# A two-block fp32 transformer kernel: norm squares behind the splits at the start, operand sums issued amid the last block's first tiles, and a compressed-key tile laid out for unit-step reads

## The chip, the cores and the metric
The kernel runs on one core of one Trainium2 chip. The metric is the device time of one execution in microseconds, the median of three runs.

## The reference
One sequence of 512 tokens with 1024 features, fp32, passes through two blocks.
```
first_block:
x = x + 0.5 * swiglu(rms_norm(x, norm_ffn1), ffn1_w1, ffn1_w3, ffn1_w2)
x = x + hybrid_mixer(rms_norm(x, norm_mix), ...)
x = x + memory_attention(rms_norm(x, norm_mem_q), rms_norm(mem, norm_mem_kv), ...)
x = x + 0.5 * swiglu(rms_norm(x, norm_ffn2), ...)
x = rms_norm(x, norm_out)
...
swiglu(h, w1, w3, w2) = (silu(h @ w1) * (h @ w3)) @ w2
rms_norm(x, g) = x * rsqrt(mean(x * x) + EPS) * g
```
The second block runs sparse attention with 16 heads in 4 groups (over compressed, selected and windowed keys), a matrix-memory LSTM and a cross-attention side by side, merges them through an output projection, and ends with a normed feed-forward network (FFN). The compressed keys come from a small MLP over blocks of 32 successive tokens, one block every 8 tokens, 31 blocks.

## The kernel before
**Products.** Activations lie transposed, features on the 128 partitions and the 512 tokens along the row: x is eight tiles x[d]. An fp32 product with full accuracy is made of three products of split operands (`mm3`): ACT casts the operand to a rounded high part (`copy_hi`, L93, with a gain L94), DVE takes the rest (`lo`, L98, L99), and PE computes high·high, high·low and low·high. `Ctx.split` issues both; with `pin` they keep program order on their engines. The order of all else is set by the tile scheduler, by priorities that follow the order of issue. Tiles come from pools: `q` (split operands, weights), `b` (8 scratch tiles) and eight PSUM banks (`ps`).

**Weights.** `Stream` loads raw weight tiles of 512 KB in the order of their use and splits them ahead. `Stream.start` loads x and the first four weight tiles together, in four pieces of two feature chunks each: per piece x[d], the columns of four raw tiles (L249), x[d + 1]; the first two of the odd ones go through ACT's queue, all else through SP's. It returns one function per piece that splits its columns. `tile_block` calls these, and `next_pair` splits x[d] and x[d + 1] with the norm's gain; the norm's own scale (one over the root of the mean square of a token) is applied behind the products, from the row tile `rb`.

**Norm.** `Norm.add_fast` squares a tile on ACT (L284) and adds it to an accumulator on DVE (L286). `finish` sums over partitions by products with ones, reads the sums into `nv` on DVE (L314), takes the root on POOL (L322) and builds diagonals on DVE (L329); products with ones spread them over the partitions, and ACT copies the result to `rb` (L334).

**FFN up.** `UpPairs` forms pairs of products by Strassen's scheme, with seven products of half size in place of eight; it needs sums and differences of the operands' halves, which `Operands.sums` makes (two scalings on ACT, L374 and L375, three adds on DVE, L377 to L379, then a split, for each of four pairs of tiles). The first tiles need no sums: `UpPairs.first` computes four plain products in the first FFN, chunk by chunk. In the last block it computes six, each in two halves of 256 tokens, since the second half of the residual stream isn't ready when the first is; `run` issues `ops.sums()` behind `first`.

**Ahead of the last FFN.** `product(h, d)` is the output projection of half h, `resid` and `resid2` form the norm and the residual sums and split the operands of the half; `rows(t, j)` transposes x back to token rows on PE (four transposes into a bank, L118), copies the bank on ACT (L2266) and stores it to `xtd`, for the end of the kernel. The object `halves` in `first` walks through these stages; its last call is the transposes of the second half.

**Compression.** `Nsa.take_c` multiplies a projected PSUM tile by the token scale `rb` and writes it into the tile `cz` for k or v (L1550, eight multiplies each); `compress` runs the MLP's first layer, 16 `k.mm` for each of k and v, whose moving operand is every eighth column of `cz` from column c on (4 groups by 31 blocks). These fp32 products are not split, and the trace shows two records for each, 64 in all.

Of the kernel before, what the change touches and what calls it, by code (L numbers as in the profile page):

```python
# [11 lines left out]
AF = mybir.ActivationFunctionType  # L12
# [3 lines left out]
P = 128  # L16
S = 512
NT = S // P
D = 1024
KD = D // P  # L20
# [16 lines left out]
class Ctx:  # L37
# [70 lines left out]
    def mm(self, out, a, b, start, stop, skip=False):  # L108
        return self.nc.tensor.matmul(out, a, b, start=start, stop=stop, skip_group_check=skip)  # L109
# [22 lines left out]
class Stream:  # L132
# [20 lines left out]
    def add(self, key, src, split=True):  # L153
        self.order.append((key, src, split))
# [79 lines left out]
    def start(self, x, xT, gains):  # L234

        k = self.k
        raw, hl = [], []
        m = 4
        for n in range(m):
            raw.append(k.rawp.tile([P, 1024], F32, tag="raw", name=k.nm("raw")))  # L240
            hl.append((k.q([P, 1024], F32R), k.q([P, 1024], F32R)))
            self.hl[n] = hl[n]
        self.nd = self.ns = self.nsum = m
        k.nc.scalar.dma_start(gains, k.a["gains"])
        for d in range(0, KD, 2):
            c = slice(d * P, (d + 2) * P)
            k.nc.sync.dma_start(x[d], xT[d])
            for n in range(m):
                (k.nc.scalar if d == 0 and n % 2 == 0 else k.nc.sync).dma_start(raw[n][:, c], self.order[n][1][:, c])  # L249
                if n == 1:  # L250
                    k.nc.sync.dma_start(x[d + 1], xT[d + 1])
        self._dma()
        return [lambda c=slice(d * P, (d + 2) * P): [k.split(hl[n][0][:, c], hl[n][1][:, c], raw[n][:, c], pin=True) for n in range(m)]
                for d in range(0, KD, 2)]

    SUMS = 2

    def next(self, key):
        self.prefetch(self.AHEAD)
        assert self.order[self.n][0] == key, (key, self.order[self.n][0])  # L260
        r = self.hl.pop(self.n)
        self.n += 1
        return r
# [9 lines left out]
class Norm:  # L273
# [4 lines left out]
        self.acc = k.b([P, cols])  # L278
        self.first = True

    def add_fast(self, x):
        k = self.k
        t = self.acc if self.first else k.b([P, self.cols])
        k.nc.scalar.activation(t, x, AF.Square)  # L284
        if not self.first:
            k.nc.vector.tensor_add(self.acc, self.acc, t)  # L286
        self.first = False
# [59 lines left out]
class Operands:  # L347
# [8 lines left out]
        self.k = k  # L356
        self.b1, self.b2, self.th, self.tl, self.x = [], [], [], [], []

    def add(self, x1, x2, g1, g2, c=slice(0, S), pin=False):

        k = self.k
        if c.start == 0:
            self.b1.append(k.q([P, 2, S], F32R))
            self.b2.append(k.q([P, 2, S], F32R))
            self.x.append((x1, x2, g1, g2))
        j = next(j for j in range(KD // 2) if self.x[j][0] is x1)
        for b, x, g in ((self.b1[j], x1, g1), (self.b2[j], x2, g2)):
            k.split(b[:, 0, c], b[:, 1, c], x[:, c], g, pin)

    def sums(self):  # L370
        k, nc, H = self.k, self.k.nc, self.H
# [45 lines left out]
class UpPairs:  # L417
# [93 lines left out]
    def first(self):  # L511


        k, halves = self.k, self.halves
        ps = []
        if halves is None:
            for n in range(self.side):
                ps.append((k.ps(), self.weights(0, "ab"[n // 2])[n % 2]))
            for kk in range(KD):
                for p, w in ps:  # L520
                    self.plain(p, w, ks=[kk])
            return [p for p, _ in ps]
        for n in range(self.side):
            ps.append((k.ps(), self.weights(n // 4, "ab"[n // 2 % 2])[n % 2]))
            if n in (1, 2):
                halves = halves()
            self.plain(*ps[n], slice(0, 256))
        for n, (p, w) in enumerate(ps):
            self.plain(p, w, slice(256, 512))
            if n == 1:  # L530
                last = self.finish()
            if n == 3:
                self.rb = last()
        halves()
        return [p for p, _ in ps]

    def run(self):
        k = self.k
        steps = up_steps()
        which = {1: "x", 6: "x", 7: "x", 4: "x", 5: "y", 3: "y", 2: "z"}  # L540
        done = {"a": "a", "b": "b", 4: "a22", 3: "s34", 5: "s12", 2: "f1"}
        last = None
        pend = []
        ps0 = self.first()
        self.ops.sums()
        for n, num in steps:
            if ps0:
                ps, ps0 = ps0[:2], ps0[2:]
                pend.append((n, num, ps))
            elif num in ("a", "b"):  # L550
                ps = [k.ps(), k.ps()]
                for m, (p, w) in enumerate(zip(ps, self.weights(n, num))):
                    self.plain(p, w)
                    if m == 0 and last is None and self.rb is None:
                        last = self.finish()
                pend.append((n, num, ps))
            else:
                first = num in (1, 5, 2)
                if first:
                    self.bank[n, which[num]] = k.ps([P, 2, 256])  # L560
                self.product(n, num, self.bank[n, which[num]], first)
                self.take(n, num)
            if self.rb is None and last is not None:
                self.rb = last()
            if self.rb is not None:
                while pend:
                    m, ab, ps = pend.pop(0)
                    self.out_plain(2 * m + (ab == "b"), *ps)
                if (n, 11) in self.c:
                    z = self.c.pop((n, 11))  # L570
                    self.out(2 * n, 0, z, z)
            if n == NF // 2 - 1:
                k.W.AHEAD = 2
                if num == 1:
                    self.ops.b1 = None
                if num == 4:
                    self.ops.th = self.ops.tl = None
            if num in done:
                self.w.pop((n, done[num]), None)
        k.W.AHEAD = Stream.AHEAD  # L580
        self.ops.b2 = None
        return self.g
# [39 lines left out]
    norm.add(x[d])  # L622


def next_pair(x, ops, d, gain, norm, pin=False):
    ops.add(x[d], x[d + 1], gain[:, d : d + 1], gain[:, d + 1 : d + 2], pin=pin)
    if not pin:
        norm.add(x[d])
        norm.add(x[d + 1])

# [875 lines left out]
class Nsa:  # L1506
# [34 lines left out]
    def take_c(self, which, c):  # L1541
        def take(p):
            k, nc = self.k, self.k.nc
            if c == 0:
                self.cz[which] = k.q([P, 4, 256])
            z = self.cz[which]
            for j in range(2):
                r = slice(64 * j, 64 * j + 64)
                for par in range(2):
                    nc.vector.tensor_mul(z[64 * par : 64 * par + 64, 2 * c + j, :], p[r, par::2], self.rb[r, par::2])  # L1550
        return take

    def compress(self):

        k, nc = self.k, self.k.nc
        w1, acc = {}, {}
        for which in "kv":
            w1[which] = [k.q([P, 1024]) for _ in range(2)]
            for hf in range(2):
                nc.sync.dma_start(w1[which][hf], k.a["cmp_w1_" + which][hf])  # L1560
        for which in "kv":
            acc[which] = k.b([P, P])
            self.pe_sum(nc.gpsimd if which == "k" else nc.vector, which, w1[which], acc[which])
        for which in "kv":
            z = self.cz.pop(which)
            w = w1.pop(which)
            p = k.ps([P, 4, 32])
            for c in range(16):
                k.mm(p[:, :, :31], w[c // 8][:, (c % 8) * P : (c % 8 + 1) * P], z[:, :, c : c + 241 : 8], c == 0, c == 15)
                yield 216  # L1570
            pb = k.ps([P, 2])
            k.mm(pb[:, 0:1], acc.pop(which), k.ones[:, 0:1], True, True)
            hid = self.hidden(p, pb)
            yield 3000
            self.second(which, hid)
            yield 1000
# [309 lines left out]
def tile_block(ctx: ExitStack, tc: tile.TileContext, aps, out):  # L1886
    nc = tc.nc
    k = Ctx(ctx, tc, aps)
# [38 lines left out]
    G = {n: gains[:, i, :] for i, n in enumerate(GAINS)}  # L1927
    x = [k.half() for d in range(KD)]
    k.warm(12)
    first = W.start(x, aps["xT"], gains)  # L1930
# [10 lines left out]
    k.rb = k.const([P, S], "rb")  # L1941
    ops, norm = Operands(k), Norm(k)
    for d in range(0, KD, 2):
        first[d // 2]()
        next_pair(x, ops, d, G["norm_ffn1"], norm, True)
    for d in range(KD):
        norm.add_fast(x[d])
    x.clear()

    up = UpPairs(k, ("ffn1_w1", "ffn1_w3"), ops, lambda norm=norm: norm.finish(None, k.rb), 4)  # L1950
# [1 line left out]
    g = up.run()  # L1952
# [3 lines left out]
    xs, norm = [], Norm(k)  # L1956
    for d, p in ffn_down(k, "ffn1_w2", g):
        t = k.b()
# [28 lines left out]
    xs, norm = [], Norm(k)  # L1987
# [35 lines left out]
    ops, norm = Operands(k), Norm(k)  # L2023
# [10 lines left out]
    g = up.run()  # L2034
# [5 lines left out]
    xs, norm, norm5 = [], Norm(k), Norm(k)  # L2040
    for d, p in ffn_down(k, "ffn2_w2", g):
        t = k.b()
# [451 lines left out]
```

## Time and profile before
| | before |
|---|---|
| median of three runs | 2230.64 us (2230.48 to 2231.96) |
| profiled execution | 2232.27 us |
| its span | 2230.5 us |
| mean granted clock of TensorE | 0.995 |
| busy: PE, weight loads, DVE, ACT, POOL | 2192.0, 1911.3, 1515.2, 1021.4, 297.7 us |
| DMA | 235.73 MB, 106 GB/s in mean |

PE is the matrix engine, DVE the vector engine, ACT the scalar engine, POOL the general one, and SP issues most DMAs. A busy time counts records on the engine; PE's is near the span, so time is gained only where PE waits or where its records become shorter. Where records overlap at their ends, a count in a stretch includes those cut by its edges.

### The profile page before, as it was taken

What the parts mean: (1) busy time and instruction counts of PE and PEld (TensorE: products, weight loads), DVE (VectorE), ACT (ScalarE), POOL (GpSimd) and SP (SyncE); (2) the same over time, 40 slices, a digit from 0 to 9 for tenths busy, and PEclk for the clock granted to TensorE, in tenths of its full rate; (3) what the DMA queues carried; (4) which work ended last, traced back from release to release, by engine and by line L of the source; (5) the groups of instructions that cost most, each with busy time, mean ns of one, the idle gap of its engine ahead of it and who ended that gap; (6) DMA issues with size and microseconds to landing.
All of it is one profiled execution on the core that took longest, in us unless ns stands there. A gap on an engine that the chain in (4) does not pass through costs nothing.

```text
span 2230.5 us, 32697 instructions
## 1 busy us (share of the span) xinstructions
PE 2192.0 (98%) x12746; PEld 1911.3 (86%) x12746; DVE 1515.2 (68%) x2601; ACT 1021.4 (46%) x1790; POOL 297.7 (13%) x347
## 2 busy tenths in 40 slices
PE   8999999999999999999999999999999999899998
PEld 6999888878888889999888878887777799899987
DVE  7898644656866667888445945626888747798832
ACT  6455523545344544545224443315666635554620
POOL 0000021301234030000230000213334200000000
PEclk9999999999999999999999999999999999999999
DMA  5233524212333332335133223531111442233431
GB/s 175 95 114 99 180 66 140 74 64 83 124 124 104 114 109 81 104 114 187 54 118 133 67 91 100 180 122 58 58 48 58 142 152 95 76 114 104 160 105 38
DMA packets 79076, 235.73 MB, mean 106 GB/s; under 512 B 9028, under 2 KB 12868, under 8 KB 78920
## 3 DMA queue, kind: packets, MB, share of 16 engines
q1 hardware_dynamic: 74456, 225.99, 30.9%
q10 hardware_dynamic: 4464, 7.65, 0.9%
q8 instruction: 100, 1.64, 0.3%
q14 instruction: 56, 0.46, 0.1%
HBM read 216.30 MB, written 17.30 MB: 105 GB/s over the span
## 4 chain that ended last, share of the span: by engine, by line
PE 88%; DVE 6%; ACT 2%; issue 2%; POOL 1%; DMA 0%; SPq 0%; ACTq 0%; DVEq 0%; POOLq 0%
PE ps L109 86%; PE ps L118 2%; DVE q L98 1%; ACT q L1755 1%; DVE nx L1753 1%; POOL hr L322 1%; DVE q L99 0%; ACT q L93 0%; DMA raw<-in_ffn_w_dram 0%; DVE b L286 0%; DVE q L2245 0%; DVE q L1653 0%; DVE hn L723 0%; DVE nr L1757 0%; POOL q L1760 0%
## 5 line engine op out<-in xcount | busy, mean ns | idle before, releaser
L109 PE MATMUL ps<-q,q 128*128 128x256 f32 (+3 forms) x11736 | 2119.0, 341 | 19.9 <-ACT q L94 8.9
L109 PEld LDWEIGHTS ps<-q,q 128*128 128x128 f32 x11736 | 1803.9, 191 | 254.2 <-ACT q L94 9.1
L98 DVE TENSOR_TENSOR q<-raw,q 128x1024 fp32r<-128x1024 f32 (+2 forms) x385 | 430.3, 1135 | 101.8 <-ACT q L93 54.7
L93 ACT CAST q<-raw 128x1024 fp32r<-128x1024 f32 (+2 forms) x385 | 349.6, 938 | 111.3 <-PE ps L109 88.6
L93 ACT CAST q<-q 128x1024 fp32r<-128x1024 f32 (+1 forms) x188 | 164.8, 892 | 139.2 <-PE ps L109 66.0
L98 DVE TENSOR_TENSOR q<-q,q 128x1024 fp32r<-128x1024 f32 (+1 forms) x188 | 189.5, 1025 | 57.1 <-ACT q L93 49.7
L293 POOL TENSOR_TENSOR b<-q 128x512 f32<-128x512 f32 x32 | 36.9, 1156 | 709.4 <-DVE q L1960 302.5
L468 ACT ACTIVATE b<-b 128x256 f32<-128x256 f32 x108 | 44.9, 417 | 134.5 <-DVE b L467 134.5
L1755 ACT ACTIVATE q<-ps,nx 128x128 f32<-128x128 f32 (+3 forms) x128 | 67.5, 531 | 56.9 <-DVE nx L1753 25.7
L1760 POOL TENSOR_SCALAR q<-q,nr 128x128 f32<-128x128 f32 (+3 forms) x128 | 72.0, 569 | 143.7 <-DVE nr L1758 99.7
L459 ACT COPY b<-ps 128x512 f32<-128x512 f32 x81 | 47.3, 584 | 90.1 <-PE ps L109 90.0
L118 PE MATMUL ps<-ident,q 128*128 128x128 f32 x512 | 81.6, 275 | 6.7 <-POOL q L1760 2.6
L118 PEld LDWEIGHTS ps<-ident,q 128*128 128x128 f32 x512 | 61.9, 141 | 25.0 <-POOL q L1760 8.0
L98 DVE TENSOR_TENSOR q<-ps,q 128x512 fp32r<-128x512 f32 x112 | 74.1, 682 | 11.2 <-ACT q L93 10.8
L94 ACT ACTIVATE q<-q,gains 128x512 fp32r<-128x512 f32 (+1 forms) x48 | 30.4, 648 | 105.2 <-DVE q L1960 34.6
L297 POOL TENSOR_TENSOR b<-b,b 128x512 f32<-128x512 f32 (+1 forms) x49 | 70.6, 1447 | 2.8
L93 ACT CAST q<-ps 128x512 fp32r<-128x512 f32 x112 | 62.7, 593 | 16.8 <-PE ps L109 11.6
L1753 DVE TENSOR_REDUCE nx<-ps 128x1 f32<-128x384 f32 (+3 forms) x96 | 56.0, 583 | 0.0
L99 DVE SCALAR_TENSOR_TENSOR q<-q,gains,q 128x512 fp32r<-128x512 f32 (+1 forms) x48 | 35.5, 753 | 19.2 <-ACT q L94 19.1
L322 POOL TENSOR_TENSOR sr<-ss,mhalf 128x4 f32<-128x4 f32 x8 | 8.1, 1008 | 296.5 <-DVE ss L1387 187.3
L469 DVE TENSOR_TENSOR q<-b,b 128x256 f32<-128x256 f32 x81 | 33.8, 421 | 19.4 <-ACT b L468 19.0
L322 POOL TENSOR_TENSOR or<-ov,mhalf 128x1 f32<-128x1 f32 x4 | 2.2, 548 | 334.4 <-DVE ov L2345 334.4
(264 smaller groups left out, 1417.7 us busy)
## 6 DMA issues: line engine op xcount, KB each, us to landing
raw<-in_ffn_w_dram SPq DMA_DIRECT2D x100, 512.0 KB, 4.3
raw<-in_w_ffn_in_dram SPq DMA_DIRECT2D x44, 512.0 KB, 3.8
raw<-in_w_gm_dram SPq DMA_DIRECT2D x24, 512.0 KB, 3.3
raw<-in_ffn_w2a_dram SPq DMA_DIRECT2D x22, 512.0 KB, 4.4
raw<-in_w_ffn_down_dram SPq DMA_DIRECT2D x22, 512.0 KB, 4.4
raw<-in_w_out_dram SPq DMA_DIRECT2D x16, 512.0 KB, 3.6
raw<-in_w_mk_dram SPq DMA_DIRECT2D x8, 512.0 KB, 3.6
raw<-in_w_mv_dram SPq DMA_DIRECT2D x8, 512.0 KB, 4.0
```

What stands on the lines that cost most here:

```text
L93: return self.nc.scalar.copy(out, in_)
L98: return self.nc.vector.tensor_sub(out, in_, hi.bitcast(F32))
L99: return self.nc.vector.scalar_tensor_tensor(out, in_, gain, hi.bitcast(F32), op0=ALU.mult, op1=ALU.subtract)
L109: return self.nc.tensor.matmul(out, a, b, start=start, stop=stop, skip_group_check=skip)
L118: return self.nc.tensor.transpose(out, in_, self.ident[:n, :n])
L293: k.nc.gpsimd.tensor_tensor(t, x, x, op=ALU.mult)
L297: k.nc.gpsimd.tensor_tensor(self.acc, self.acc, t, op=ALU.add)
L459: self.k.nc.scalar.copy(z, bank)
L468: nc.scalar.activation(t, t, AF.Silu)
L1753: nc.vector.tensor_reduce(mx, s.rearrange("p j b t -> p b j t"), axis=AX.XY, op=ALU.max, negate=True)
L1755: nc.scalar.activation(pr[b][:, :n], s[:, :, c, :], AF.Exp, bias=mx[:, c : c + 1], accum_out=sm[:, c : c + 1])
L1760: nc.gpsimd.tensor_scalar(pr[b][:, :n], pr[b][:, :n], r[:, c : c + 1], 1.0, op0=ALU.mult, op1=ALU.mult)
```

## The change
Four pieces of code change.

- At the start, the first two feature chunks become pieces of their own (cuts 0-1, 1-2, 2-4, 4-6, 6-8); `next_pair` hands a function down through the argument `pin`, so that the second chunk's weight columns are split between the two x tiles. The squares of the first norm are pinned, which puts them in program order, behind all splits.
- `UpPairs.first` of the last block calls the transposes behind the second half of tile 0 and drops its weights tile by tile.
- `ops.sums()` of the last block is issued behind the second half of tile 1.
- `cz` has the layout [4, 8, 32] in place of [4, 256]: token 8n + r lies at row r, place n. The multiplies write with a step of 32 elements, and the first layer reads 31 successive ones.

```diff
@@ Stream.start
-        for d in range(0, KD, 2):
-            c = slice(d * P, (d + 2) * P)
-            k.nc.sync.dma_start(x[d], xT[d])
+        cuts = [(0, 1), (1, 2), (2, 4), (4, 6), (6, 8)]
+        for a, b in cuts:
+            c = slice(a * P, b * P)
+            k.nc.sync.dma_start(x[a], xT[a])
             for n in range(m):
-                (k.nc.scalar if d == 0 and n % 2 == 0 else k.nc.sync).dma_start(raw[n][:, c], self.order[n][1][:, c])
-                if n == 1:
-                    k.nc.sync.dma_start(x[d + 1], xT[d + 1])
+                (k.nc.scalar if a == 0 and n % 2 == 0 else k.nc.sync).dma_start(raw[n][:, c], self.order[n][1][:, c])
+                if n == 1 and b == a + 2:
+                    k.nc.sync.dma_start(x[a + 1], xT[a + 1])
...
@@ Operands.add
-        for b, x, g in ((self.b1[j], x1, g1), (self.b2[j], x2, g2)):
-            k.split(b[:, 0, c], b[:, 1, c], x[:, c], g, pin)
+        k.split(self.b1[j][:, 0, c], self.b1[j][:, 1, c], x1[:, c], g1, pin is not None)
+        if pin is not None:
+            pin()
+        k.split(self.b2[j][:, 0, c], self.b2[j][:, 1, c], x2[:, c], g2, pin is not None)
@@ UpPairs.first
-        for n, (p, w) in enumerate(ps):
+        for n in range(self.side):
+            p, w = ps[n]
             self.plain(p, w, slice(256, 512))
+            ps[n] = p, None
+            if n % 2 == 1:
+                del w, self.w[n // 4, "ab"[n // 2 % 2]]
+            if n == 0:
+                halves()
             if n == 1:
                 last = self.finish()
+                self.ops.sums()
             if n == 3:
                 self.rb = last()
-        halves()
@@ UpPairs.run
-        self.ops.sums()
+        if self.halves is None:
+            self.ops.sums()
@@ Nsa.take_c
-                self.cz[which] = k.q([P, 4, 256])
+                self.cz[which] = k.q([P, 4, 8, 32])
...
-                    nc.vector.tensor_mul(z[64 * par : 64 * par + 64, 2 * c + j, :], p[r, par::2], self.rb[r, par::2])
+                    nc.vector.tensor_mul(z[64 * par : 64 * par + 64, 2 * c + j].rearrange("p r n -> p n r"),
+                                         p[r, par::2].rearrange("p (n r) -> p n r", r=8),
+                                         self.rb[r, par::2].rearrange("p (n r) -> p n r", r=8))
@@ Nsa.compress
-                k.mm(p[:, :, :31], w[c // 8][:, (c % 8) * P : (c % 8 + 1) * P], z[:, :, c : c + 241 : 8], c == 0, c == 15)
+                k.mm(p[:, :, :31], w[c // 8][:, (c % 8) * P : (c % 8 + 1) * P], z[:, :, c % 8, c // 8 : c // 8 + 31], c == 0, c == 15)
@@ tile_block
-        first[d // 2]()
-        next_pair(x, ops, d, G["norm_ffn1"], norm, True)
+        first[d]()
+        next_pair(x, ops, d, G["norm_ffn1"], norm, first.get(d + 1, lambda: None))
     for d in range(KD):
-        norm.add_fast(x[d])
+        norm.add_fast(x[d], True)
```

The scheduler turns this into an order on each engine. ACT at the start of the program, before (raw are weight tiles, q_80 to q_82 tiles of x):
```order
L249 DMA raw_97<-in_ffn_w_dram 128x256
L249 DMA raw_103<-in_ffn_w_dram 128x256
L284 ACT_TABLE_LOAD
L284 ACTIVATE b_141<-q_80 128x512
L284 ACTIVATE b_199<-q_80 128x512
L284 ACTIVATE b_202<-q_81 128x512
L284 ACTIVATE b_205<-q_81 128x512
L284 ACTIVATE b_208<-q_82 128x512
L93 CAST q_98<-raw_97 128x256
L93 CAST q_101<-raw_100 128x256
L284 ACTIVATE b_211<-q_82 128x512
L93 CAST q_104<-raw_103 128x256
```
and now:
```order
L250 DMA raw_97<-in_ffn_w_dram 128x128
L250 DMA raw_103<-in_ffn_w_dram 128x128
L93 ACT_TABLE_LOAD
L93 CAST q_98<-raw_97 128x128
L93 CAST q_101<-raw_100 128x128
L93 CAST q_104<-raw_103 128x128
L93 CAST q_107<-raw_106 128x128
L94 ACTIVATE q_154<-q_80,gains 128x512
L93 CAST q_98<-raw_97 128x128
L93 CAST q_101<-raw_100 128x128
L93 CAST q_104<-raw_103 128x128
L93 CAST q_107<-raw_106 128x128
```
The five squares (L284) ahead of the first cast are gone, the casts are half as wide, and the first scaling of x comes behind the first four.

DVE at the read of the first norm's sum (`nv`; q_384 and q_388 belong to the third of four operand sums, b_473 and b_485 are the diagonals), before:
```order
L378 TENSOR_TENSOR q_384<-b_380,q_384 128x256
L379 TENSOR_TENSOR q_384<-b_381,q_384 128x512
L314 TENSOR_SCALAR nv_445<-ps_440 128x4
L329 TENSOR_SCALAR b_473<-ident,nr_447 128x128 x3
L98 TENSOR_TENSOR q_389<-q_384,q_388 128x1024
```
and now:
```order
L383 TENSOR_TENSOR q_384<-b_380,q_384 128x256
L384 TENSOR_TENSOR q_384<-b_381,q_384 128x512
L317 TENSOR_SCALAR nv_457<-ps_452 128x4
L332 TENSOR_SCALAR b_485<-ident,nr_459 128x128 x4
L98 TENSOR_TENSOR q_389<-q_384,q_388 128x1024
```
The read stands behind the same sum as before, and all four diagonals now come in one piece.

ACT at the last block's operand sums (b_18175 and b_18077 are their first scaled operands, b_18144 and the like the transposed rows, rb the norm's scale), before:
```order
L93 CAST q_17914<-raw_17781 128x1024
L334 COPY rb<-ps_18084 128x256
L334 COPY rb<-ps_18091 128x256
L2266 COPY b_18144<-ps_18143 128x512
L2266 COPY b_18152<-ps_18151 128x512
L2266 COPY b_18160<-ps_18159 128x512
L2266 COPY b_18168<-ps_18167 128x512
L374 ACTIVATE b_18175<-q_16201,gains 128x512
L375 ACTIVATE b_18176<-q_17070,gains 128x512
```
and now:
```order
L2281 COPY b_18022<-ps_18021 128x512
L2281 COPY b_18030<-ps_18029 128x512
L379 ACTIVATE b_18077<-q_16213,gains 128x512
L380 ACTIVATE b_18078<-q_17082,gains 128x512
L379 ACTIVATE b_18089<-q_17082,gains 128x512
L380 ACTIVATE b_18090<-q_17085,gains 128x512
L379 ACTIVATE b_18101<-q_17085,gains 128x512
L380 ACTIVATE b_18102<-q_17088,gains 128x512
L93 CAST q_18085<-q_18081 128x1024
L379 ACTIVATE b_18113<-q_17088,gains 128x512
L380 ACTIVATE b_18114<-q_17091,gains 128x512
L337 COPY rb<-ps_18176 128x256
```
The copies of the norm's scale stood ahead of the row copies and the scalings; now the scalings and the first split of a sum stand ahead of the scale.

## Rows read from the trace of the kernel before
**Rows 1.** The page's busy times by engine, and its chain by engine
```profile
PE 2192.0 (98%) x12746; PEld 1911.3 (86%) x12746; DVE 1515.2 (68%) x2601; ACT 1021.4 (46%) x1790; POOL 297.7 (13%) x347
...
PE 88%; DVE 6%; ACT 2%; issue 2%; POOL 1%; DMA 0%; SPq 0%; ACTq 0%; DVEq 0%; POOLq 0%
```

**Rows 2.** Waits of PE: what released it, total us, times, mean us
```profile
PE ps L109 <- ACT q L94: 8.9, 1, 8.9
PE ps L109 <- DVE q L98: 3.9, 4, 2.5
```

**Rows 3.** Timeline, 0 to 45: start, us, engine, line, operation, out<-in, count [idle before <-releaser]
```profile
11.50 0.69 ACT L93 CAST q<-raw 128x256 fp32r<-128x256 f32 x2
14.48 29.38 PE L109 MATMUL ps<-q,q 128*128 128x512 f32 x120 [8.92 <-ACT q L94]
```

**Rows 4.** Timeline of PE, 1862 to 1935, the last block's start
```profile
1886.35 6.00 PE L109 MATMUL ps<-q,q 128*128 128x256 f32 x48
1901.55 16.93 PE L109 MATMUL ps<-q,q 128*128 128x512 f32 x96 [0.24 <-ACT b L2266]
1921.17 0.74 PE L109 MATMUL ps<-q,q 128*128 128x256 f32 x4 [2.69 <-ACT q L93]
1924.46 10.73 PE L109 MATMUL ps<-q,q 128*128 128x256 f32 x69 [2.54 <-DVE q L98]
```

**Rows 5.** Windows and lines by form of PE, 1432.6 to 1446.9 (compression)
```profile
1432.60:1446.90 14.30, 14.30 (x64) 12.44 (x63) 4.34 (x5) 2.20 (x3) 1.43 (x2) 1.00 0.64 207
L109 PE MATMUL ps<-q,q 128*128 128x124 f32 x32 | 9.0, 398 | 0.0
```

**Rows 6.** Lines by form of PE, 1470 to 1500
```profile
L109 PE MATMUL ps<-q,q 128*128 128x512 f32 x134 | 30.5, 389 | 0.0
```

**Rows 7.** Chain, 0 to 60: start us, us, what
```profile
1.66 5.06 DMA raw<-in_ffn_w_dram
```

**Rows 8.** Lines by form, 0 to 24.5: count | busy us, mean ns | idle before
```profile
L98 DVE TENSOR_TENSOR q<-raw,q 128x256 fp32r<-128x256 f32 x16 | 5.8, 417 | 0.0
L99 DVE SCALAR_TENSOR_TENSOR q<-q,gains,q 128x512 fp32r<-128x512 f32 x8 | 5.6, 745 | 0.0
L94 ACT ACTIVATE q<-q,gains 128x512 fp32r<-128x512 f32 x8 | 5.3, 714 | 0.0
L93 ACT CAST q<-raw 128x256 fp32r<-128x256 f32 x16 | 5.3, 398 | 0.0
```

**Rows 9.** Windows: us, PE, PEld, DVE, ACT, POOL busy (records), PEclk, DMA share, GB/s
```profile
16.00:18.00 2.00, 2.00 (x6) 1.56 (x5) 2.00 (x6) 2.00 (x5) 0.00 (x0) 0.50 0.99 360
1926.00:1930.00 4.00, 4.00 (x23) 4.00 (x23) 3.95 (x5) 0.97 (x2) 0.00 (x0) 0.56 0.37 132
```

**Rows 10.** Timeline, 36 to 80: the first norm's scale and the operand sums
```profile
39.04 0.69 DVE L379 TENSOR_TENSOR q<-b,q 128x512 f32<-128x512 f32 x1
45.00 1.02 POOL L322 TENSOR_TENSOR nr<-nv,mhalf 128x4 f32<-128x4 f32 x1 [44.15 <-DVE nv L314]
50.10 1.06 PE L109 MATMUL ps<-b,ones 128*128 128x128 f32 x8
50.91 29.28 PE L109 MATMUL ps<-q,q 128*128 128x512 f32 x199
59.91 1.22 DVE L98 TENSOR_TENSOR q<-q,q 128x1024 fp32r<-128x1024 f32 x1
```

**Rows 11.** Timeline of ACT and DVE, 1895 to 1930
```profile
1901.87 0.73 ACT L374 ACTIVATE b<-q,gains 128x512 f32<-128x512 f32 x1
1923.19 1.22 DVE L98 TENSOR_TENSOR q<-q,q 128x1024 fp32r<-128x1024 f32 x1
```

**Rows 12.** Lines by form and timeline of DVE, 1394 to 1432; PE by form, 1409.2 to 1410
```profile
L1550 DVE TENSOR_TENSOR q<-ps,rb 64x256 f32<-64x256 f32 x16 | 6.8, 422 | 4.1 <-PE ps L109 3.9
1399.46 1.73 DVE L1550 TENSOR_TENSOR q<-ps,rb 64x256 f32<-64x256 f32 x4
L109 PE MATMUL ps<-q,q 128*128 128x124 f32 x4 | 1.1, 402 | 0.0
```

More of the change, by code (lines that the diff above doesn't have):

```diff
@@ L244, in start @@
         k.nc.scalar.dma_start(gains, k.a["gains"])
-        for d in range(0, KD, 2):
-            c = slice(d * P, (d + 2) * P)
-            k.nc.sync.dma_start(x[d], xT[d])
+        cuts = [(0, 1), (1, 2), (2, 4), (4, 6), (6, 8)]
+        for a, b in cuts:
+            c = slice(a * P, b * P)
+            k.nc.sync.dma_start(x[a], xT[a])
             for n in range(m):
-                (k.nc.scalar if d == 0 and n % 2 == 0 else k.nc.sync).dma_start(raw[n][:, c], self.order[n][1][:, c])
-                if n == 1:
-                    k.nc.sync.dma_start(x[d + 1], xT[d + 1])
+                (k.nc.scalar if a == 0 and n % 2 == 0 else k.nc.sync).dma_start(raw[n][:, c], self.order[n][1][:, c])
+                if n == 1 and b == a + 2:
+                    k.nc.sync.dma_start(x[a + 1], xT[a + 1])
         self._dma()
-        return [lambda c=slice(d * P, (d + 2) * P): [k.split(hl[n][0][:, c], hl[n][1][:, c], raw[n][:, c], pin=True) for n in range(m)]
-                for d in range(0, KD, 2)]
+        return {a: lambda c=slice(a * P, b * P): [k.split(hl[n][0][:, c], hl[n][1][:, c], raw[n][:, c], pin=True) for n in range(m)]
+                for a, b in cuts}
     SUMS = 2
@@ L279, in __init__, with add_fast @@
         self.first = True
-    def add_fast(self, x):
+    def add_fast(self, x, pin=False):
         k = self.k
         t = self.acc if self.first else k.b([P, self.cols])
-        k.nc.scalar.activation(t, x, AF.Square)
+        a = k.nc.scalar.activation(t, x, AF.Square)
+        if pin:
+            k.tc.keep_in_program_order(a)
         if not self.first:
@@ L357, in __init__, with add @@
         self.b1, self.b2, self.th, self.tl, self.x = [], [], [], [], []
-    def add(self, x1, x2, g1, g2, c=slice(0, S), pin=False):
+    def add(self, x1, x2, g1, g2, c=slice(0, S), pin=None):
         k = self.k
@@ L622, in next_x, with next_pair @@
     norm.add(x[d])
-def next_pair(x, ops, d, gain, norm, pin=False):
+def next_pair(x, ops, d, gain, norm, pin=None):
     ops.add(x[d], x[d + 1], gain[:, d : d + 1], gain[:, d + 1 : d + 2], pin=pin)
-    if not pin:
+    if pin is None:
         norm.add(x[d])
```

## The prediction
> **What bounds the kernel now.** I read the page first: PE is busy for 2192.0 of 2230.5 us and holds 88% of the chain that ended last [rows 1]. So only three things can pay: a wait of PE, a stretch at the lower clock, or records that take longer than their columns need. The list of PE's waits, one releaser per row, gives the first: 8.9 us in one piece on a scaled x chunk of ACT, and behind it a pile of 3.9 us on splits of DVE [rows 2]. By the timeline they have two places: the wait of 8.92 us ahead of the first product, at 14.48 [rows 3], and in the last block the waits of 2.69 us ahead of 1921.17 and 2.54 us ahead of 1924.46 [rows 4]. The change touches both, and a third place where PE never waits: the compression, whose 124-column records are looked at by form [rows 5].
>
> The measure for a plain product: 134 records of 512 columns took 30.5 us, 0.2276 us each [rows 6]; one of 256 columns at that rate is 0.114, and 48 of them in the last block took 6.00, 0.125 each with edges [rows 4].
>
> **Part A, the start.** ACT runs five squares, each behind the DMA of an x tile, ahead of its first weight cast (the first of the order's pieces); the cast starts at 11.50 and the first product at 14.48 [rows 3]. Now no square stands there, and the first chunk is one tile of 128 rows (128 columns of the raw tiles) instead of two. Its pieces: the chain shows a first 128 KB piece issued at 1.66 that took 5.06 us, landing at 6.72 [rows 7]. The new pieces are half as large, but four more transfers are issued and all share the engines. Bounds for the landing of the last piece needed: 4.5 (issue, and about half of that time) and 6.72; I take 5.6. Behind it come a cast of at most 0.398 and the x scale of 0.714 [rows 8]: the first product at 6.7 instead of 14.48, **−7.8 us** (bounds −6.7 and −8.9).
>
> PE isn't starved behind it: a pair of chunks is 24 products, 24 × 0.2276 = 5.5 us, and its splits on ACT take 4 × 0.398 + 2 × 0.714 = 3.0 us, on DVE 4 × 0.417 + 2 × 0.745 = 3.2 us [rows 8]. The first single chunk pays some more fixed time in 128-column casts, inside the same cover. The next x and weight pieces have 2.7 us per chunk; if they come late, the gain falls, and this is rival 1's ground.
>
> [...] The 120 first products took 29.38 us [rows 3] against 120 × 0.2276 = 27.3, so half clock and the wait for the first rest cost 2.1 us together. The earlier start has the same kind of stretch ahead of it (PE's warm-up on the ones tile, then idle, now shorter). I keep 2.1; it may be 0 (a gain of 2 more) or twice as much.
>
> What is late next: the norm's scale. Squares and adds moved behind the splits, and the read of the norm's sum on DVE still stands behind the third operand sum (second of the order's pieces), which started at 39.04 and takes 0.69 [rows 10]. DVE isn't earlier there, since it does the same work: 39.7 to 40.7 with seven adds moved behind the splits. Then come POOL's root of 1.02 us and some 0.6 for the read and the first diagonal (an estimate from the same stretch): 41.4 to 42.3, with three more diagonals behind. PE asks for them at 50.10 − 7.8 = 42.3 [rows 10]: 0 to 0.8 us lost, and I take 0.8. The last piece of the operand-sum chain, a split of 1.22 us that started at 59.91, ends at 61.1 [rows 10]; PE used it after 48 products of 512 and 64 of 256 columns behind the diagonals' 8, at 50.9 + 10.9 + 7.3 = 69.1, so now at 61.3, with DVE up to 1 us later: 0.7 lost. After that PE's operands lead by 5 us and more, as weights come from the stream. **A = −7.8 + 0.8 + 0.7 = −6.3 us**, bounds −3 (both chains late by twice that and the landing at 6.72) and −9.5.
>
> **Part B, the last block.** The gap at 1921 to 1927 is the operand sums': their first multiply on ACT starts at 1901.87, behind the row copies, and the chain ends with the split at 1923.19 + 1.22 = 1924.4, 22.5 us later [rows 11]. PE, after 96 products in 16.93 us from 1901.55, has nothing else: it waits 2.69, does 4 records, waits 2.54, and then runs 69 records in 10.73 us, where 69 × 0.125 = 8.6 would do [rows 4]; 2.1 us of half clock [rows 9] behind the idle time. The change issues the sums after the second tile, so ACT's multiplies come ahead of the norm's row copies (third of the order's pieces), at about 1887 when PE works on the 48 records from 1886.35. The chain then ends near 1909.5 at the same 22.5 us, and is wanted at 1918.5 (1901.55 + 16.93): 9 us to spare. The transposes go in amid the first tiles; the small wait of 0.24 behind them goes [rows 4]. The row scale comes later on ACT by eight multiplies and a cast, some 8 × 0.73 + 1.05 = 7 us, around 1900, before the first tile of the next pairs must leave its bank. I cost that at nothing; its cover is the two PSUM banks that the six tiles leave free. **B = −2.69 − 2.54 − 2.1 − 0.2 = −7.5 us**, bounds −3 (part of the wait comes back elsewhere) and −8.5.
>
> **Part C, the compression.** 64 records of 124 columns read every eighth element. In 1432.60 to 1446.90 PE did 32 of them and 32 products of 512 columns without a pause [rows 5]: 14.30 − 32 × 0.2276 = 7.0 us, 0.219 each, nearly the time of 512 columns. The nearest unit-step records of the same type, 128 columns of a diagonal against ones, took 8 in 0.81 us until the next product started at 50.91, 0.101 each [rows 10]. So 0.107 (between this and 0.114) may be reached: 64 × (0.219 − 0.107) = **−7.2 us**, bounds 0 (the step isn't the cause) and −7.6 (0.101 each).
> [...]
>
> That half: the 16 multiplies that write the tile, 0.422 us each [rows 12], now write with a step of 32 elements. No row of this kernel shows a DVE write with such a step. Bounds: 0 more, and, if they doubled as the strided reads of PE do here (0.219 against 0.107), 0.42 more each. The first tile's last four end at 1401.2, and PE's first read of it falls between 1409.2 and 1410 [rows 12]: 8 us of lead for a pass of eight, which takes 8 × 0.42 = 3.4 us more at the upper bound. It lies beside PE; I take 0 on the path.
> [...]
>
> **Sum.** −6.3 − 7.5 − 7.2 = −21.0. The profiled execution took 2232.27 us (span 2230.5); it would take 2211.3. The median of the runs shown is 1.63 us lower, 2230.64, so the forecast is **2209.6 us**.
>
> **Rivals.**
> - *The start's gain is given back inside the first FFN* (DMA pieces land late, or the norm chain and PSUM banks hold PE at 42 to 62 us). For it: the norm's read still stands behind the operand sums, and squares are later. Against: 3.0 us of splits to 5.5 us of products. A is −3 instead of −6.3: about 2213. Chance 0.15.
> - *The step isn't what makes the 124-column records long* (each is two passes over full rows, or bound by its weight load). Against: the 128-column records at 0.101 load weights too. C is 0: 2216.8. Chance 0.08.
> - *The last block's gap only moves*: transposes amid the tiles hold PE at copies of ACT, or the later row scale holds a bank. B is −3: 2214. Chance 0.07.
> - *The clock stays low* through the first 96 products, because PE starts dense work at once after a short warm-up. The half-clock window shows 6 records in 2.00 us, of which the edges cut two [rows 9], so 0.33 to 0.50 each, and I take 0.43: 96 × (0.43 − 0.23) − 2.1 = 17 more, 2226.7, within the noise or a little better. Chance 0.03.
> - *Slower: the strided writes of DVE end on the path.* With e more for each, a pass waits on PE's side from 8 e = 8, and the two together cost 16 e − 16. Against the 21 gained, that is slower by over 4.5 us from e = 2.6. At ten times the old price, e = 3.8: 16 × 3.8 − 16 = 45, less 21, 24 on top of 2230.6, about 2254. For it: a pattern that no row shows. Against: PE's own step of eight cost a factor of two, not ten. Chance 0.03.
>
> **How the numbers follow.** The main case has 0.64. The first, third and most of the second rival lie within 2209.6 + 7.2. The low end takes the landing at 4.5 and no loss behind it (−2.5), a full recovery of the clock (−2) and −1.5 of C and B: 2203.5. The high end, 2217.5, takes in the second rival. Outside are the last two rivals and sums of misses. A measurement of this kernel can tell some 0.2%, 4.5 us, from no change: all cases but the last two are faster by more, and the clock's is within it. So faster 0.94, same 0.03, slower 0.03.
>
> **What would show it.** In the changed profile: a first 512-column product near 6.7 us, and the list of waits without the 8.9; the diagonals' products near 43 us and no gap above 1 us until 70; in the last block the operand sums' multiplies 15 us earlier, with no wait near the old 1921 and no half-clock window behind; 124-column records near 0.107 in a stretch without pauses, and the take-multiplies at 0.42 to 0.85. The forecast is wrong if PE starts after 9 us, if the granted clock stays at 0.50 past 20 us, or if the 124-column records keep 0.219.

## The result and the profile after

The changed kernel takes **2211.47 us** in the median of four runs (2209.04 to 2212.11), beside 2231.27 us for the kernel before: a ratio of 0.9909, 95% interval 0.9892 to 0.9927. A second set on another occasion gave 2210.30 and 0.9902 (0.9887 to 0.9917). The forecast was 2209.6, range 2203.5 to 2217.5.

The profiled execution took 2209.04 us (span 2207.2, mean granted clock 0.999), the fastest of its four, so its span is 23.3 us shorter than the one before, while the medians differ by 19.8. Part of the difference between executions is read off a second profile below. The page's busy times and chain of the changed kernel, answering to [rows 1]:

```profile
PE 2182.1 (99%) x12746; PEld 1902.7 (86%) x12746; DVE 1518.6 (69%) x2605; ACT 1021.0 (46%) x1794; POOL 299.0 (14%) x347
...
PE 84%; DVE 8%; ACT 3%; issue 2%; POOL 2%; DMA 1%; SPq 0%; POOLq 0%; DVEq 0%; ACTq 0%
```

DVE has 3.4 us more, and its share of the chain rose from 6% to 8%: PE is still the bound, but DVE holds it at more places.

PE at the start, in the timeline of the changed kernel (start, us, engine, line, operation, count, in brackets the idle time before and what ended it), answering to [rows 3, 10]:

```profile
1.05 5.49 PE L109 MATMUL ps<-ones 128*128 128x128 f32 x24 [1.05 <-DVE ones L1907]
6.37 6.64 PE L109 MATMUL ps<-q,q 128*128 128x512 f32 x25
13.30 21.84 PE L109 MATMUL ps<-q,q 128*128 128x512 f32 x95 [0.29 <-DVE q L99]
34.97 0.95 PE L109 MATMUL ps<-ones,b 128*128 128x1 f32 x8
35.78 5.75 PE L109 MATMUL ps<-q,q 128*128 128x512 f32 x24
41.37 1.06 PE L109 MATMUL ps<-b,ones 128*128 128x128 f32 x8
42.18 22.68 PE L109 MATMUL ps<-q,q 128*128 128x512 f32 x144
66.72 8.53 PE L109 MATMUL ps<-q,q 128*128 128x256 f32 x69 [1.86 <-ACT b L464]
```

The first product stands at 6.37, straight behind the warm-up, and in this execution no row waits for the norm: the diagonals' products at 41.37 have no bracket (a second profile, below, has one). A new wait stands at 66.72, 1.86 us for a copy of ACT (L464) that empties a PSUM bank.

The last block and the compression in the timeline of the same execution, answering to [rows 4, 5], and the multiplies that write the compressed tile (lines by form), answering to [rows 12]:

```profile
1874.96 6.00 PE L109 MATMUL ps<-q,q 128*128 128x256 f32 x48
...
1882.08 30.10 PE L109 MATMUL ps<-q,q 128*128 128x256 f32 x206
...
1387.59 25.74 PE L109 MATMUL ps<-q,q 128*128 128x512 f32 x128
1413.85 0.38 PE L109 MATMUL ps<-ones,b 128*128 128x1 f32 x2 [0.51 <-POOL b L1606]
...
L1563 DVE TENSOR_TENSOR q<-ps,rb 64x256 f32<-64x256 f32 x16 | 10.1, 633 | 1.7 <-PE ps L109 1.5
```

In the last block one row of 206 products runs from 1882.08 to 1912.2, the end of the stretch that was read, without a bracket: both waits and the slow 69 records are gone. In the compression 128 products (32 of them of 124 columns) take 25.74 us; the same row of the kernel before reads:

```profile
1394.24 29.46 PE L109 MATMUL ps<-q,q 128*128 128x512 f32 x128
```

That is 3.72 us less for 32 records, 0.116 each. The multiplies became longer, 0.633 us instead of 0.422, and at 1413.85 PE now waits 0.51 us for an add of POOL (L1606).

Putting PE's records of both traces side by side, the same record of each, gives the lead of the changed kernel, by how many us it is ahead at that record:

| PE's record | before | after | lead |
|---|---|---|---|
| first product | 14.48 | 6.37 | 8.1 |
| first product behind the norm's diagonals | 50.91 | 42.18 | 8.7 |
| first product of the bank that is waited for | 73.43 | 66.72 | 6.7 |
| start of the first compression stretch | 1394.24 | 1387.59 | 6.7 |
| the record behind it | 1423.54 | 1413.85 | 9.7 |
| the 96 products ahead of the old gap | 1901.55 | 1887.43 | 14.1 |
| the 69 records behind the old gap | 1924.46 | 1904.57 | 19.9 |
| end of the span | 2230.5 | 2207.2 | 23.3 |

From 9.7 to 14.1 lie the second compression stretch (3.7) and the last block's transposes, whose two waits near 1900 are gone (0.7). Behind the old gap 2.3 us more come from the records that no longer run at half clock (a granted clock near 0.50: 0.50 from 1924.4 to 1926 and 0.56 from 1926 to 1930 before, 1.00 from 1904.5 to 1912 now), and the last 1.1 from the end of the kernel: the span ended 3.7 us behind the issue of the final store before, and 2.6 now. The kernel with the compression alone has 3.6 there and the one with the start alone 2.6; no run shows why.

### The profile page after: what moved, and what is told of

The parts are those of the page before. It is cut to its first block, busy times and chain, and to the rows that moved or that the text cites. A ratio compares the mean times of both kernels' runs of the same rounds, so it can differ in the third digit from the quotient of the medians.

```text
span 2207.2 us, 32709 instructions
## 1 busy us (share of the span) xinstructions
PE 2182.1 (99%) x12746; PEld 1902.7 (86%) x12746; DVE 1518.6 (69%) x2605; ACT 1021.0 (46%) x1794; POOL 299.0 (14%) x347
## 4 chain that ended last, share of the span: by engine, by line
PE 84%; DVE 8%; ACT 3%; issue 2%; POOL 2%; DMA 1%; SPq 0%; POOLq 0%; DVEq 0%; ACTq 0%
PE ps L109 82%; PE ps L118 2%; DVE q L98 2%; ACT q L93 1%; ACT q L1770 1%; DVE nx L1768 1%; POOL hr L325 1%; DVE q L99 0%; DMA raw<-in_ffn_w_dram 0%; ACT b L285 0%; DVE q L1668 0%; DVE b L289 0%; DVE q L2260 0%; DVE q L1563 0%; POOL q L1601 0%
## 5 line engine op out<-in xcount | busy, mean ns | idle before, releaser
L98 DVE TENSOR_TENSOR q<-raw,q 128x1024 fp32r<-128x1024 f32 (+3 forms) x389 | 429.6, 1122 | 97.5 <-ACT q L93 55.5
L93 ACT CAST q<-raw 128x1024 fp32r<-128x1024 f32 (+3 forms) x389 | 351.0, 931 | 106.9 <-PE ps L109 69.4
L464 ACT COPY b<-ps 128x512 f32<-128x512 f32 x81 | 47.3, 584 | 83.7 <-PE ps L109 83.7
L99 DVE SCALAR_TENSOR_TENSOR q<-q,gains,q 128x512 fp32r<-128x512 f32 (+1 forms) x48 | 35.6, 754 | 19.9 <-ACT q L94 19.1
```

What stands on the lines that cost most here:

```text
L93: return self.nc.scalar.copy(out, in_)
L98: return self.nc.vector.tensor_sub(out, in_, hi.bitcast(F32))
L99: return self.nc.vector.scalar_tensor_tensor(out, in_, gain, hi.bitcast(F32), op0=ALU.mult, op1=ALU.subtract)
L464: self.k.nc.scalar.copy(z, bank)
```

## The experiments

The theory was that the three parts add up and that the start gives some 2 us back at the wait for the bank's copy. The rivals: that a part's gain depends on the others, or that later waits take the start's gain back whole.

**Each part alone.** The start alone takes the diff's pieces in `Stream.start`, `add_fast`, `Operands.add`, `next_pair` and `tile_block`:

```diff
+        cuts = [(0, 1), (1, 2), (2, 4), (4, 6), (6, 8)]
...
+        norm.add_fast(x[d], True)
```


> The kernel before with the change of the start alone (cuts, squares behind the splits). Theory: the parts add up, so the first product stands near 6.4 us instead of 14.48 and PE runs 8 to 9 us ahead until 60 us; about 2 are given back at the wait for a bank's copy near 66, and the rest, 6.5 us, lasts to the end: a profile span of some 2224, a ratio of 0.997. Rival: later waits take the whole gain back (ratio 0.999 or more), and the other two parts carry the result.

Measured: 2226.13 us against 2231.57, ratio 0.9976 (0.9965 to 0.9987), 5.4 us. The span of the profile, 2225.7, shows only 4.8, and 1.1 of these are the final store's. PE's first product stands at 6.79, and 8.0 us of lead are kept to the diagonals; then the wait for the bank, 2.34 us, costs more than in the changed kernel's first profile. Windows of this kernel (us, busy of PE, PEld, DVE, ACT, POOL with records, PEclk, DMA share, GB/s):

```profile
66.00:68.00 2.00, 0.00 (x0) 0.00 (x0) 1.49 (x3) 2.00 (x3) 0.00 (x0) 1.00 0.00 0
68.00:70.00 2.00, 1.77 (x12) 1.77 (x13) 2.00 (x4) 1.22 (x3) 0.00 (x0) 0.81 0.04 8
70.00:72.00 2.00, 2.00 (x11) 2.00 (x11) 2.00 (x4) 1.02 (x1) 0.00 (x0) 0.50 0.00 0
72.00:74.00 2.00, 2.00 (x17) 2.00 (x16) 2.00 (x5) 1.14 (x3) 0.00 (x0) 0.83 0.71 213
```

PE is idle for all of 66 to 68, and behind it the granted clock is 0.50 from 70 to 72: 2.9 us of lead go at the diagonals (0.3) and with the wait, and 1.5 with the half clock, 4.4 of the 8.0. The theory had the place right and only 2 us for it, so its 6.5 us came out as 5.4; the rival, all of the gain, falls.

The last block alone takes the pieces in `UpPairs.first` and `run`:

```diff
+            if n == 0:
+                halves()
             if n == 1:
                 last = self.finish()
+                self.ops.sums()
```


> The kernel before with the change of the last block alone (transposes amid the first tiles, sums behind tile 1). Theory: the two waits of 2.69 and 2.54 us and the half-clock window behind them go, 8 to 9 us in all, span some 2222, ratio 0.996. Rival: the gap was closed in the changed kernel by the earlier parts (weights further ahead), so that alone this part gives 5 us or less.

Measured: 2221.95 us, ratio 0.9955 (0.9941 to 0.9970), 9.6 us. PE's row in the timeline to 1930, with no wait inside:

```profile
1894.77 35.50 PE L109 MATMUL ps<-q,q 128*128 128x256 f32 x251
```

The part stands by itself; the rival (that weights further ahead had helped) falls.

The compression alone takes the pieces in `take_c` and `compress`:

```diff
-                k.mm(p[:, :, :31], ..., z[:, :, c : c + 241 : 8], c == 0, c == 15)
+                k.mm(p[:, :, :31], ..., z[:, :, c % 8, c // 8 : c // 8 + 31], c == 0, c == 15)
```


> The kernel before with the compressed tile's layout alone. Theory: 64 records go from 0.219 to 0.122 us in the flow of PE, 6.2 us, ratio 0.997, with the multiplies at 0.63 instead of 0.42 us and no wait of PE for them. Rival: the longer multiplies keep DVE 3.4 us busier and a later wait of PE gives half of the gain back, 3 us in all.

Measured: 2225.28 us, ratio 0.9971 (0.9960 to 0.9982), 6.3 us, the theory's size. Its price for a record mixes two measures, though: side by side, PE gains 3.7 us in each of the two stretches (0.116 a record, not 0.097) and loses 0.5 at a wait of 0.19 for POOL's add, where the theory had no wait. The three single gains sum to 21.3 us, against 19.8 and 21.9 in the two timed sets of the whole change: they add up within the intervals.

**What closed the last block's gap.** Two kernels take one of its two moves back.

```diff
             if n == 1:
                 last = self.finish()
-                self.ops.sums()
...
-        if self.halves is None:
-            self.ops.sums()
+        self.ops.sums()
```


> The changed kernel with the operand sums issued behind the first tiles again, as before; the transposes stay amid the tiles. Theory: it was the issue of the sums that closed the gap, so PE waits some 5 us again near 1907 and the span is 8 us longer, 2215. Rival: the sums were held by the scratch tiles that the row copies took ahead of them, and with the transposes moved they run early even when issued late: no gap, span 2207 to 2209.

```diff
-            if n == 0:
-                halves()
...
+        halves()
         return [p for p, _ in ps]
```


> The changed kernel with the transposes of the second half behind the first tiles again, the sums issued behind tile 1. Theory: since moving the transposes alone closed the gap, what matters is that the sums' scratch tiles aren't taken behind those of the row copies; issuing the sums ahead of them does that as well, so no gap near 1905 and a span of 2207 to 2210. Rival: the late transposes hold PE at the row copies (0.3 to 0.5 us) or the sums still come late, and 5 us or more return.

Measured, one run of each: spans of 2210.0 and 2208.9 (both with the longer wait near 67 that is treated below), and no gap in either. The rows of PE in the first and in the second kernel:

```profile
1884.30 30.94 PE L109 MATMUL ps<-q,q 128*128 128x256 f32 x213
```

```profile
1886.21 1.03 PE L118 MATMUL ps<-ident,q 128*128 128x128 f32 x8
1887.54 1.14 PE L118 MATMUL ps<-ident,q 128*128 128x128 f32 x8 [0.29 <-ACT b L2280]
1888.92 26.29 PE L109 MATMUL ps<-q,q 128*128 128x512 f32 x174 [0.24 <-ACT b L2280]
```

So either move alone closes the gap, and my theory for the first of the two (that the issue of the sums is what counts) was wrong: with the transposes moved, the sums' first scaling starts at 1875.45 though it is issued later. What both moves have in common shows in ACT's order: the sums' scalings no longer stand behind late row copies. Before, the copies ran from 1899.53 and the first scaling at 1901.87; in the first kernel the copies are early too, from 1872.59, and the scalings begin at 1875.45; in the second the scalings begin at 1869.95 and the copies come at 1886.90. That it was the scratch tiles which put the scalings behind the copies is argued, since a kernel with more scratch tiles wasn't tried. Late transposes still cost their two waits of 0.29 and 0.24.

**The step.** Two layouts between the old and the new:

```diff
-                self.cz[which] = k.q([P, 4, 8, 32])
+                self.cz[which] = k.q([P, 4, 4, 32, 2])
```


> The changed kernel with the compressed tile as [4, 4, 32, 2]: PE reads every second element (8 bytes apart), DVE writes pairs. [...] Rival: any step costs, 0.17 or more.

The second has [P, 4, 2, 32, 4] in that place.

> The changed kernel with the compressed tile as [4, 2, 32, 4]: PE reads every fourth element (16 bytes apart). [...] Rival: the cost grows with the step, and four gives something between 0.122 and 0.219.

The stretch of 128 products and the writing multiplies with a step of two, then of four:

```profile
1388.89 25.81 PE L109 MATMUL ps<-q,q 128*128 128x512 f32 x128
...
L1563 DVE TENSOR_TENSOR q<-ps,rb 64x256 f32<-64x256 f32 x16 | 6.8, 422 | 4.1 <-PE ps L109 3.9
```

```profile
1391.04 29.30 PE L109 MATMUL ps<-q,q 128*128 128x512 f32 x128
...
L1563 DVE TENSOR_TENSOR q<-ps,rb 64x256 f32<-64x256 f32 x16 | 6.8, 422 | 4.1 <-PE ps L109 3.9
```

A step of two costs what unit steps cost (25.81 against 25.74); a step of four costs nearly what eight did (29.30 against 29.46). The rivals fall: the cost doesn't grow with the step, it is there in full at 16 bytes and absent at 8 (12 wasn't run). Why is not shown. On DVE's side writes in pairs or fours cost the old 0.422 us, and single elements 128 bytes apart 0.633.

**What gives the start's gain back.** The chain in the changed kernel runs over DVE, which works nearly without a pause from 40.40 to 63, and over ACT, which does two casts ahead of the copy (chain of the changed kernel, 40 to 70: start, us, what):

```profile
40.40 0.87 DVE b L332 x4
...
60.52 2.27 DVE q L98 x2
62.79 0.61 DVE b L501
...
64.21 1.97 ACT q L93 x2
66.18 0.49 ACT b L464
...
66.72 3.37 PE ps L109 x26
```

The first attempt took work off both engines:

```diff
-        norm.add_fast(x[d], True)
+        norm.add(x[d])
```


> The changed kernel with the first norm's squares and adds on POOL, which is idle there, instead of ACT (8 x 0.63 us) and DVE (7 x 0.69 us). Theory: what gives the start's gain back is DVE, which works without a pause from 40 to 63 us, and ACT's bank copy behind it; with 4.8 us less on DVE and 4.3 on ACT the sums start some 4 us earlier, the wait of 1.9 to 2.3 us near 67 and the half-clock stretch that follows it in some executions go, and the time is 2 to 4 us below the changed kernel: about 2208, ratio 0.990 to 0.989. Rival: PE waits for the weights or the norm's sum instead (POOL needs 8 x 1.16 + 7 x 1.45 = 19.4 us, its last add may end after 35 us, when PE asks for it), so the time stays at 2211 or rises.

Measured: 2221.12 us, ratio 0.9954 (0.9940 to 0.9967), 10 us worse than the changed kernel. The rival had the outcome (PE waits, and the time rises), but neither it nor the theory named the cause: POOL's last add ended at 26.9, long before PE asked for it, at 40.64. Lines by form from 8 to 26 in this kernel:

```profile
L98 DVE TENSOR_TENSOR q<-raw,q 128x256 fp32r<-128x256 f32 x9 | 11.9, 1375 | 0.1
...
L300 POOL TENSOR_TENSOR b<-b,b 128x512 f32<-128x512 f32 x7 | 10.1, 1439 | 0.5
...
L99 DVE SCALAR_TENSOR_TENSOR q<-q,gains,q 128x512 fp32r<-128x512 f32 x5 | 7.1, 1460 | 0.0
...
L93 ACT CAST q<-raw 128x256 fp32r<-128x256 f32 x12 | 4.6, 402 | 3.5 <-DMA raw<-in_ffn_w_dram 3.4
```

and the same two DVE lines in the changed kernel, 5 to 20:

```profile
L99 DVE SCALAR_TENSOR_TENSOR q<-q,gains,q 128x512 fp32r<-128x512 f32 x8 | 5.7, 749 | 0.7 <-DMA raw<-in_ffn_w_dram 0.5
...
L98 DVE TENSOR_TENSOR q<-raw,q 128x256 fp32r<-128x256 f32 x12 | 4.5, 422 | 2.0 <-ACT q L93 2.0
```

While POOL works, DVE's rests take 1.375 us instead of 0.422 and 1.460 instead of 0.749; ACT's casts stay at 0.40. PE then waits for DVE, first for the rests of x (5.5 us behind the changed kernel at 24.40) and then for the diagonals, in three pieces (6.7 more):

```profile
16.04 7.07 PE L109 MATMUL ps<-q,q 128*128 128x512 f32 x24 [2.64 <-DVE q L99]
...
49.71 1.20 PE L109 MATMUL ps<-b,ones 128*128 128x128 f32 x4 [2.52 <-DVE b L332]
```

POOL had time to spare, but DVE's operations took longer beside its work there. Behind POOL's last add the old time is back: the two operations of L99 that start at 28.15 take 1.40 us together. How the one lengthens the other is not shown.

The second attempt came from the pieces at the start: it keeps the squares behind the splits and goes back to the old cuts.

```diff
-        cuts = [(0, 1), (1, 2), (2, 4), (4, 6), (6, 8)]
+        cuts = [(0, 2), (2, 4), (4, 6), (6, 8)]
```


> The changed kernel with the old cuts of two chunks each; the squares stay behind the splits. Theory: the squares ahead of the first cast were the larger part, so the first product stands near 8.5 us (pieces of 128 KB that land at 6.7 to 7.5, a cast and a scale), 2 later than 6.4. Rival: the piece size decides, first product near 12.

Measured: one time of 2207.27, first product at 7.36; in a second profile (the timed runs below) it stands at 8.15. So the squares were 6.3 to 7.1 of the 8.1 us, and the single chunks the other 1.0 to 1.8, which isn't kept. The kernel was timed beside two others:

> The changed kernel with the old cuts, timed. Theory: the single-chunk pieces gain 1.0 us at the first product, but with them the scheduler puts all four diagonals of the first norm in one piece on DVE, which waits 1.2 us there for POOL's root, and DVE carries that to the bank copy near 66 us; the old cuts are 2 to 4 us faster, 2207 to 2209. Rival: the one look was a lucky execution, and the median is 2211 like the changed kernel's.

> The changed kernel once more, beside the two above on the same chip. Theory: 2211, and in its profile a wait of 1.9 to 2.4 us for the bank copy near 67, with a stretch at the half clock behind it where the wait is the longer. Rival: the spread of its times comes from the clock at the start, and the wait is the same in each.

> The changed kernel with the old cuts and the tile as [4, 4, 32, 2]. Theory: the step of two gives DVE 3.4 us back and leaves PE's records nearly as they are, so the time is that of the old cuts alone within 1 us, 2207 to 2209, below both kernels. Rival: DVE's 3.4 us stood on the path somewhere, and it is 2 us faster than the old cuts alone.

| kernel | median us (range) | ratio to before (interval) |
|---|---|---|
| changed, again | 2210.30 (2208.86 to 2211.91) | 0.9902 (0.9887 to 0.9917) |
| old cuts | 2209.30 (2208.28 to 2210.46) | 0.9897 (0.9883 to 0.9912) |
| old cuts, step of two | 2207.22 (2207.18 to 2207.58) | 0.9889 (0.9872 to 0.9905) |

The timeline of the second (old cuts) around the norm, and its bank copy:

```profile
40.24 1.23 DVE L98 TENSOR_TENSOR q<-q,q 128x1024 fp32r<-128x1024 f32 x1 [1.04 <-ACT q L93]
41.38 0.42 DVE L382 TENSOR_TENSOR q<-b,b 128x256 f32<-128x256 f32 x1
41.72 0.28 DVE L332 TENSOR_SCALAR b<-ident,nr 128x128 f32<-128x128 f32 x1
...
45.38 0.68 DVE L213 TENSOR_TENSOR q<-raw 128x512 f32<-128x512 f32 x1
...
61.78 6.40 PE L109 MATMUL ps<-q,q 128*128 128x256 f32 x52
...
65.29 0.57 ACT L464 COPY b<-ps 128x512 f32<-128x512 f32 x1
```

The scheduler places the last split and sum between the diagonals (L332) here, while in the changed kernel DVE waits 1.21 us for POOL's root at 40.40 ahead of all four; DVE's next work (L213) starts at 45.38 instead of 46.18 and the copy at 65.29 instead of 66.09, while PE's products behind the diagonals start 1.7 us later (43.84 instead of 42.18), and PE doesn't wait near 67. So of the wait of 1.86 us, 0.8 at most went because DVE is earlier, and the larger part because PE arrives later; the order of the diagonals wasn't changed by itself. Behind the bank PE is 0.4 us ahead of the changed kernel's first profile and 1.8 ahead of its second. As times, old cuts and changed kernel can't be told apart.

The second profile of the changed kernel (2211.91 us) gives more of the start back. DVE reads the norm's sum at 40.46 instead of 39.04, PE waits 0.93 us for the diagonals, and the copy starts at 67.53 instead of 66.09, with a wait of 2.33 us for the bank and a stretch at half clock behind it:

```profile
42.26 1.13 PE L109 MATMUL ps<-b,ones 128*128 128x128 f32 x8 [0.93 <-DVE b L332]
...
70.00:72.00 2.00, 2.00 (x11) 2.00 (x11) 2.00 (x5) 1.05 (x1) 0.00 (x0) 0.50 0.00 0
```

PE's lead falls here from 8.9 to 7.8 at the diagonals, to 5.3 at the bank and to 3.7 behind the stretch: 5.2 us are given back, against 2.1 in the first profile. That is the 2.9 us between the two spans; why DVE comes 1.4 us later is not shown. With a wait of 1.86 us there was no stretch at half clock (the granted clock of the first profile is 1.00 from 66 to 76). But a longer wait doesn't always bring one: six profiles have a wait of 2.33 to 2.35 us here, and five of them the stretch. The kernel with the step of two waits 2.35 and keeps the clock:

```profile
70.00:72.00 2.00, 2.00 (x19) 2.00 (x18) 2.00 (x5) 1.27 (x2) 0.00 (x0) 1.00 0.00 0
```

What decides it stays open. The rival, the clock at the start, falls for these two profiles: in both the granted clock is 1.00 from 4 to 16.

With the step of two as well, DVE's multiplies are at 0.422 again, and PE's row behind the compression has no wait (in the kernel of the old cuts alone it waits 0.99 for POOL's add, L1606):

```profile
1386.27 25.81 PE L109 MATMUL ps<-q,q 128*128 128x512 f32 x128
1411.92 0.28 PE L109 MATMUL ps<-ones,b 128*128 128x1 f32 x2
```

```profile
1387.13 25.75 PE L109 MATMUL ps<-q,q 128*128 128x512 f32 x128
1413.87 0.38 PE L109 MATMUL ps<-ones,b 128*128 128x1 f32 x2 [0.99 <-POOL b L1606]
```

So the longer multiplies did stand on the path, as the rival of that run had it, with 1.1 of the 2.2 us between these two profiles. The rest is mostly clock: from 461 to 465 it was 0.59 with the old cuts and 1.00 here (1.4 us of lead), and from 10 to 12 it was 1.00 with the old cuts and 0.50 here (1.6 us the other way); neither edit explains either. At 2207.22 us, with no run above 2207.58, this version is below every run of the changed kernel. The single earlier run of the old cuts, whose mean granted clock was 1.000, took 2207.27, so what the step of two gains on top of the old cuts isn't settled beyond that wait, 0.6 to 1.0 us.

## Why the prediction was right, and where its steps failed

The forecast of the total was 1.9 us too low, and the three parts were each of the forecast kind. That it came so close is in part luck: timed alone, the start gave 0.9 us less than forecast, the compression 0.9 less and the last block 2.1 more.

- **Start, first product.** −7.8 forecast, −8.1 measured (−7.9 in the second profile); ACT's last of the first four casts started at 5.4, so the pieces landed no later than the 5.6 taken. The rival of late pieces holds in a small way: the first 120 products take 28.8 us (6.64 + 0.29 + 21.84) instead of 27.3, for brief waits, at a granted clock of 1.00 (4 to 40).
- **Start, clock.** "I keep 2.1" of half clock was wrong: in both profiles of the changed kernel the clock is 1.00 there, and in the first 1.5 of the 2.1 came back as the brief waits. The low-clock rival had the sign wrong here, though the clock at the start isn't settled: the old cuts with a step of two ran at 0.50 from 10 to 12.
- **Start, what is given back.** The size was near in one execution (2.1 against 1.5 forecast) and too small in others (5.2 in the second profile, 4.4 for the start alone). Of the two places the diagonals were right in part: 0.8 was forecast, and PE waited 0 there in the first profile, where the read of the sum came at 39.04, ahead of the forecast 39.7 to 40.7, and 0.93 in the second, where it came at 40.46. The other place was wrong: PE never waits for the last operand sum. The step that failed is "After that PE's operands lead by 5 us and more": operands led, but PE needed an empty bank, and that hung on DVE's evictions and an ACT copy behind two casts. I had named banks in a rival and costed nothing there. A measured alone is −5.4, against −6.3 and the bound of −3; by PE's records alone, without the final store, it is −3.6.
- **Last block.** −7.5 forecast, −9.6 alone as a time; in the traces 3.0 + 2.8 + 2.3 at the gap and 0.7 ahead of it, 8.7. The terms were right but for the 0.2 at the transposes, which left out the first of two waits (0.29 ahead of 1900.16); their reason was incomplete, since either move would have done.
- **Compression.** −7.2 forecast; 3.7 in each of the two stretches, less 0.8 at POOL's add (0.51 of it the wait), 6.6; −6.3 as a time. The step that failed is small: "It lies beside PE" looked only at PE's first read of the tile, 8 us later, and not at the other work queued on DVE and POOL behind multiplies that became 0.21 us longer.
- **Rivals.** The first (the gain given back inside the first FFN, A = −3) holds in good part: its PSUM bank is the place, and the second profile keeps 3.7 us. The step as the cause was settled by steps of two and four. The slower rival needed 2.6 us more for each multiply; it was 0.21.

## What to carry to other kernels

When work starts earlier, follow each chain that doesn't start earlier (here DVE and ACT from the norm to the bank copies, which took back 2.1 to 5.2 us of the lead) to where PE catches up with it; that place, not the operands' lead, sets what is kept. Read both ends of a layout change: a step of two fp32 elements on the reading side kept the whole gain (25.81 us against 25.74 for 128 products) and spared the writing side (0.422 us a multiply against 0.633). Before moving work to an idle engine, look at what runs beside it at that time (here DVE's rests went from 0.422 to 1.375 us).

## What the runs showed of the hardware that was not expected

- Splits on DVE took 1.375 us beside POOL's squares and adds, and 0.422 without them.
- PE's records of 124 columns cost the same at a step of 8 bytes as at 4, and the full price at 16 as at 32 bytes (128 products in 25.81, 25.74, 29.30 and 29.46 us); DVE's writes of single elements 128 bytes apart cost half as much again (0.633 us against 0.422), not twice.
- A wait of 2.33 to 2.35 us on PE was followed by a stretch at half clock (granted clock 0.50 to 0.62 from 70 to 72) in five profiles of six; in the sixth, and behind a wait of 1.86 us at the same place, the clock stayed at 1.00.
